# A hybrid encoder layer on one core: statistics and scaling of sv behind earlier tiles of u, and the multiplies by gffn behind later low parts

## The chip, the cores and the metric

The kernel runs on one core of a Trainium2 chip. A core has five engines with a queue each: TensorE (PE in the profile, its weight loads PEld), VectorE (DVE), ScalarE (ACT), GpSimd (POOL) and SyncE (SP), which here only issues DMAs. Each engine takes its instructions in the order of the program; an instruction that must wait for another engine holds all that stand behind it. The metric is the device time of one execution in microseconds (us), lower is better. All times before are of the kernel as it stands in the section after next.

## The reference, cut to what matters

One layer, 512 positions of width 1024, float32. The input projection yields eight pieces; the spatial gating unit (SGU) uses two of them, u and sv:

```
proj = h @ w_in
q, k, v, g, u, sv, a_ret, a_sgu = split(proj)

# SGU branch
u  = gelu(u)
sv = layernorm(gelu(sv), sgu_ln_g, sgu_ln_b)      # over the 1024 features of a position
mixed = einsum('gpq,bnqgc->bnpgc', w_spatial, sv by chunks of 128) + b_spatial
y_sgu = (u * mixed) @ w_sgu_o

merged = sigmoid(a_ret) * y_ret + sigmoid(a_sgu) * y_sgu
x  = x + rmsnorm(merged @ w_out) * g_post_mix
h2 = rmsnorm(x) * g_pre_ffn
f  = conv_gated_mlp(h2)                            # ends with (512 x 2816) @ w_down (2816 x 1024)
y  = x + rmsnorm(f) * g_post_ffn
```

The change touches two places: the layer norm of sv (its mean, variance and scaling, without the gain and bias, which are folded in later), and the multiply of f by g_post_ffn at the end.

## The kernel before, in words

**Products in split precision.** Every float32 operand of a product is split into a high part (a copy by ScalarE, rounded to TensorE's format, L97) and a low part (source minus high part, a subtraction by VectorE, L114). Each product is three matmuls: high by high, high by low, low by high. So each 512 KB block of weights costs a DMA, a split on ScalarE, a subtraction on VectorE, and then matmuls. Where a product is a 2 x 2 block product, the kernel uses a Strassen-like scheme with seven products of sums of blocks. The sums of weights (T1 to T4 at L196 to L202, and L217 to L222 for the last product) are VectorE's and in part POOL's.

**Buffers that pace the loads.** Weights are loaded into four buffers called raw (SyncE's queue), and their parts go into nine slots (names wh, wl, wf, sh, sl, dh, dl). A raw buffer is loaded anew when the last reader of the old content is done, a slot is written anew when TensorE has used it.

**The stage of u.** Four tiles of u are whole products (`f_block`, 24 matmuls of 128 x 512, j = 0 to 3 in the loop `for j in range(UW)`); four more come as two `Pair`s of seven-product form (matmuls of 128 x 256, L915). After a whole tile VectorE multiplies it by the row scale out of PSUM (L977) and ScalarE applies the gelu (L978). In a `Pair`, `part1` makes product 0, whose result ScalarE copies to c0; product 1, which VectorE adds to c0; S1 into a third bank; then S2 on top of bank 0 (so it must wait for the copy to c0), whose result ScalarE copies to c1. `part2` adds S3 on top of bank 0 (so it waits for the copy to c1) and copies again; `part3` ends the pair.

**sv.** The eight tiles svz[t, q] (t = 0 to 3 are the position chunks, q = 0, 1 the halves of the features) are ready before the stage of u. `sv_stats` takes their statistics (two BN_STATS and a BN_AGGR for each t, on VectorE), `sv_scale` turns mean and variance into a factor and a shift (one VectorE operation, then three POOL operations on 128 x 4), and `sv_norm(q)` applies them with one ScalarE operation for each t (L715, 128 x 512). sv is next read by `mix`, in the stage of the gates after u.

**Pass two of the last product.** The product by w_down runs in two passes of 512 output features, each over nine pairs of blocks (`products(m, j)`, j = 0 to 8; 42 matmuls each, L1351). Each j needs two units of weights: "q", three of four loaded blocks as they are (128 x 768), and "t", four sums of them (128 x 1024). In pass two, after j = 2 to 5, `first_share(t)` handles a chunk of pass one's result c: two squares with row sums on ScalarE, two multiplies by gffn (names zg<-c,gpf) and the sum of the row sums (q) on VectorE. zg is next read in `rows`, in the last 15 us.

**What sets the order.** The program is recorded in the order of the code, with `w_get` recording the loads, sums and splits of weights several units ahead of their use. A scheduler then orders each engine's queue. `tc.issue_after(i)` puts what is recorded under it behind instruction i on i's engine; it adds no wait between engines.

Of the kernel before, what the change touches and what calls it, by code (L numbers as in the profile page):

```python
# [18 lines left out]
NT = S // P  # L19
# [30 lines left out]
def tile_block(ctx: ExitStack, tc, xT, x, wall, par, cs, wsp, bsp, gpost, gffn, out):  # L50
    nc = tc.nc
# [10 lines left out]
    def blk(dt=F32, n="blk", shape=(P, S)):  # L62
        return sb.tile(list(shape), dt, tag="blk", bufs=NBLK, name=nm(n))
# [17 lines left out]
    def tmp(n="tmp", shape=(P, S)):  # L81
        return sb.tile(list(shape), F32, tag="tmp", bufs=6, name=nm(n))
# [13 lines left out]
    def copy(o, i):  # L96
        return nc.scalar.activation(out=o, in_=i, func=AF.Copy)  # L97

    def two(t):
        return t.rearrange("p (n c) -> p n c", n=2)  # L100
# [5 lines left out]
    def in_turn(o):  # L106
        return o.rearrange("p (c n) -> p n c", n=2)

    def as32(t):
        return t.bitcast(F32)  # L110

    def split(hi, lo, src):
        copy(hi, src)
        nc.vector.tensor_sub(lo, src, as32(hi))  # L114

# [4 lines left out]
    i = 0  # L122
    while i < NW:
        pair = [(f, i) for f in FORMS]
        if i == SV0:
# [3 lines left out]
            i = U0  # L129
# [6 lines left out]
        elif i == UP0 + 2 * COUPLES[0][0]:  # L136
# [3 lines left out]
            i = UP0 + 2 * COUPLES[-1][1] + 2  # L140
# [10 lines left out]
    v = nc.vector  # L151
# [11 lines left out]
    def w_block(i):  # L163
        raw = raw01[i] if i < 2 else raw_tile()
        resident = RES0 <= i < RES1
        if i > 1:
            nc.sync.dma_start(raw, wall[i])
        if resident:
            hi, lo = [], []
            for c in range(2):  # L170
                h_, l_ = blk(F32R, "wh"), blk(F32R, "wl")
                split(h_, l_, raw[:, c * S : (c + 1) * S])
                hi.append(h_)
                lo.append(l_)
        else:
            at = AT_192 if i >= DOWN0 else AT_64 if UP0 <= i < UP0 + EARLY else 0
            hi, lo = slot("wh", at), slot("wl", at)
            if i < 2:
                first_blocks(i, hi, lo, raw)
            else:  # L180
                with behind():
                    split(hi, lo, raw)
        return hi, lo

    def w_form(form, i):

        if form == "B11":
            a, b = raw_tile(), raw_tile()
            nc.sync.dma_start(a, wall[i])
            nc.sync.dma_start(b, wall[i + 1])  # L190
            w_raw["B11"], w_raw["B12"] = a[:, :S], a[:, S:]
            w_raw["B22"], w_raw["B21"] = b[:, :S], b[:, S:]
        elif form == "T1":
            t = raw_tile()
            w_raw["T1"], w_raw["T2"], w_raw["T3"], w_raw["T4"] = t[:, :S], t[:, S:], w_raw["B12"], t[:, S:]
            nc.vector.tensor_add(w_raw["T1"], w_raw["B11"], w_raw["B12"])  # L196
            nc.vector.tensor_add(w_raw["T3"], w_raw["B12"], w_raw["B22"])
            eng = nc.vector if i < GATE0 or i >= UP0 else nc.gpsimd
            eng.tensor_tensor(out=w_raw["T2"], in0=w_raw["T1"], in1=w_raw["B22"], op=ALU.add)
        elif form == "T4":  # L200
            eng = nc.vector if i < GATE0 or i >= UP0 else nc.gpsimd
            eng.tensor_tensor(out=w_raw["T4"], in0=w_raw["T2"], in1=w_raw["B21"], op=ALU.add)  # L202
        w = slot("wf", 0, 1088)
        lo, hi = w[:, AT_64 : AT_64 + S], w[:, S + AT_192 : 2 * S + AT_192]
        split(hi, lo, w_raw[form])
        return hi, lo
# [507 lines left out]
    def scaled_to(t, r, o):  # L714
        nc.scalar.activation(out=t, in_=t, func=AF.Identity, scale=r, bias=o)  # L715
# [77 lines left out]
    def sv_stats(ts):  # L793
        for t in ts:
            for nh in range(2):
                v.bn_stats(out=sst[:, t, nh, :], in_=svz[t, nh])
            v.bn_aggr(out=smv[:, t, :], in_=sst[:, t].rearrange("p a b -> p (a b)"))

    def sv_scale():
        v.tensor_scalar(out=sshift, in0=smv[:, :, 0], scalar1=-1.0, scalar2=None, op0=ALU.mult)  # L800
        rsqrt(srstd, smv[:, :, 1], 1.0, NT)
        shift(sshift, srstd)

    def sv_norm(q):
        for t in range(NT):
            scaled_to(svz[t, q], srstd[:, t : t + 1], sshift[:, t : t + 1])


# [78 lines left out]
    def f_block(ah, al, n, between=None):  # L887

        wh, wl = w_get()
        o = ps()  # L890
        for k in range(n):
            if between and k == n // 2:
                between()
            c = slice(k * P, (k + 1) * P)
            mm3(o, wh[:, c], wl[:, c], turns(ah[k]), turns(al[k]), k == 0, k == n - 1)
        return o
# [76 lines left out]
    for j in range(UW):  # L973
        with tc.issue_after(summed) if j == 0 else ExitStack():
            o = f_block(xh, xl, KD)
        u = U_HOMES.pop()()
        i = v.tensor_mul(two(u), in_turn(o), two(rbc)).ins  # L977
        g = nc.scalar.activation(out=u, in_=u, func=AF.Gelu_apprx_tanh).ins  # L978
        uT.append(u)
        with tc.issue_after(i):  # L980
            sv_stats(((0, 1), (2,), (3,), ())[j])
        if j == 2:
            sv_scale()
    with tc.issue_after(g):
        sv_norm(0)
    for j in range(UW // 2, KD // 2):
        p = Pair(AF.Gelu_apprx_tanh, lambda: U_HOMES.pop()(), None, rbc)
        p.part1()
        if late:
            late.part3()  # L990
        p.part2()
        late = p
        uT += p.t
        if j == UW // 2:
            with tc.issue_after(p.copied):
                sv_norm(1)
    yh, yl = [], []

    def mix(j):
# [310 lines left out]
    i = 0  # L1310
# [100 lines left out]
    gpf = []  # L1411
    qn = [small("q", 4, 4) for _ in range(NT)]
    zg = []

    def first_share(t):
        zg.append(blk(n="zg"))
        for i in range(2):
            src = c4[2 * (t // 2) + i][:, (t % 2) * 256 : (t % 2 + 1) * 256]
            j = tmp("junk")
            nc.scalar.activation(out=j[:, :256], in_=src, func=AF.Square, scale=D ** -0.5, accum_out=qn[t][:, 2 + i : 3 + i])  # L1420
            v.tensor_mul(zg[t][:, i * 256 : (i + 1) * 256], src, gpf[0][:, i * 256 : (i + 1) * 256])
        v.tensor_add(qn[t][:, 0:1], qn[t][:, 2:3], qn[t][:, 3:4])


# [88 lines left out]
    for j in range(DP):  # L1513
        products(m, j, steps if j == DP - 1 else {}, LOOK - (j == 0), freed[0] if j == 1 else None)
        if j == 0:
            gpf.extend((hi192("gpf", F32), lo64("gpf", F32)))
            for i in range(2):
                nc.gpsimd.dma_start(gpf[i], gffn[None, i * S : (i + 1) * S].to_broadcast([P, S]))
        if 1 < j < 2 + NT:
            first_share(j - 2)  # L1520
# [136 lines left out]
```

## Time and profile before

| what | value |
|---|---|
| three executions | 785.8, 786.5, 787.52 us (median 786.5) |
| the profiled execution | 787.56 us, of which the span of its instructions 785.8 us |
| granted TensorE clock, mean | 0.997 |
| TensorE matmuls, weight loads | 777.3 us (99% of the span), 720.5 us (92%) |
| VectorE, ScalarE, POOL | 626.2 us (80%), 467.2 us (59%), 104.4 us (13%) |
| the chain that ended last | 96% of it TensorE |
| the stage of u | about 199.7 to 237 us of the span |
| pass two of the last product | about 725 to 767 us of the span |

How to read it. The columns of a timeline are start, duration, engine, source line, operation, output<-input names, sizes and count, and in brackets the idle time of the engine just before and what ended it. In a list of groups the columns after the bar are total busy time, mean duration in ns, and total idle time before them. Matmuls are pipelined: the next one starts before the one before ends, so the time between two starts says more than a duration. In a table of windows each engine's busy time stands with its count of instructions, in the order TensorE, weight loads, VectorE, ScalarE, POOL, and behind them the granted clock, the DMA share and GB/s.

### The profile page before, as it was taken

The numbers are of one execution on the slowest core, as the hardware profiler recorded it, in microseconds if no ns is written. First come the engines' busy times: TensorE is split into PE (matmuls) and PEld (weight loads), VectorE is DVE, ScalarE is ACT, GpSimd is POOL, SyncE is SP. The second block draws the span as 40 slices with busy tenths as digits, with TensorE's granted clock in tenths as the row PEclk, the third lists the DMA queues.
The fourth block names the chain that finished last, engine by engine and source line by source line (L and its number), as shares of the span: only waits on it lengthen the run. The fifth ranks groups of instructions, "written<-read, shape, count | busy, mean of one in ns | idle before, by whom it ended". The sixth has DMA issues, their size and how long they took to land.

```text
span 785.8 us, 13253 instructions
## 1 busy us (share of the span) xinstructions
PE 777.3 (99%) x5067; PEld 720.5 (92%) x5067; DVE 626.2 (80%) x1067; ACT 467.2 (59%) x848; POOL 104.4 (13%) x132
## 2 busy tenths in 40 slices
PE   9999999999999999999999999999999999999996
PEld 8888998998899999999998898999999998999996
DVE  6467987788777877867765679989999889877887
ACT  6555558689375534444444776657777578744442
POOL 0040001130011111032210210001111012200001
PEclk9999999999999999999999999999999999999998
DMA  8782224463223333223349111435555365633244
GB/s 285 268 260 90 81 81 161 108 133 128 75 82 108 108 108 108 98 92 108 134 166 330 68 68 40 122 108 141 141 148 148 108 195 115 170 114 111 103 163 161
DMA packets 35888, 104.78 MB, mean 133 GB/s; under 512 B 4400, under 2 KB 6320, under 8 KB 35824
## 3 DMA queue, kind: packets, MB, share of 16 engines
q1 hardware_dynamic: 27936, 87.81, 32.6%
q0 software_dynamic: 7024, 14.95, 9.0%
q10 hardware_dynamic: 864, 1.18, 0.4%
q8 instruction: 39, 0.64, 0.3%
q14 instruction: 25, 0.20, 0.1%
HBM read 91.34 MB, written 4.19 MB: 122 GB/s over the span
## 4 chain that ended last, share of the span: by engine, by line
PE 96%; DVE 1%; ACT 1%; issue 1%; POOLq 0%; POOL 0%; DVEq 0%; ACTq 0%
PE ps L915 21%; PE ps L289 13%; PE ps L291 13%; PE ps L290 13%; PE ps L1351 10%; PE ps L744 5%; PE ps L623 4%; PE ps L625 4%; PE ps L624 4%; PE ps L1088 2%; PE ps L1086 2%; PE ps L1087 2%; PE ps L1367 2%; PE ps L1008 1%; PE ps L409 1%
## 5 line engine op out<-in xcount | busy, mean ns | idle before, releaser
L114 DVE TENSOR_TENSOR wl<-raw,wh 128x1024 fp32r<-128x1024 f32 (+1 forms) x88 | 100.6, 1152 | 55.6 <-issue 19.1
L97 ACT ACTIVATE wf<-raw 128x512 fp32r<-128x512 f32 x126 | 75.6, 623 | 85.8 <-PE ps L290 39.8
L97 ACT ACTIVATE wh<-raw 128x1024 fp32r<-128x1024 f32 (+2 forms) x92 | 89.2, 982 | 29.1 <-DMA raw<-wall 16.8
L915 PE MATMUL ps<-sh,wf 128*128 128x256 f32 x576 | 105.8, 276 | 0.5 <-ACT u L97 0.3
L114 DVE TENSOR_TENSOR wf<-raw,wf 128x512 fp32r<-128x512 f32 x126 | 92.3, 745 | 15.2 <-ACT wf L97 14.3
L915 PEld LDWEIGHTS ps<-sh,wf 128*128 128x128 f32 x576 | 91.8, 192 | 1.7 <-ACT u L97 1.1
L289 PE MATMUL ps<-h2h,wh 128*128 128x512 f32 (+1 forms) x256 | 90.6, 354 | 0.0
L290 PE MATMUL ps<-h2l,wh 128*128 128x512 f32 (+1 forms) x256 | 90.4, 353 | 0.0
L291 PE MATMUL ps<-h2h,wl 128*128 128x512 f32 (+1 forms) x256 | 90.4, 353 | 0.0
L915 PE MATMUL ps<-sl,wf 128*128 128x256 f32 x288 | 79.2, 275 | 0.0
L1351 PE MATMUL ps<-dl,fh 128*128 128x256 f32 x216 | 59.7, 276 | 0.3 <-DVE dl L114 0.3
L1351 PE MATMUL ps<-dh,fh 128*128 128x256 f32 x216 | 59.4, 275 | 0.0
L1351 PE MATMUL ps<-dh,fl 128*128 128x256 f32 x216 | 59.4, 275 | 0.0
L915 PEld LDWEIGHTS ps<-sl,wf 128*128 128x128 f32 x288 | 55.2, 192 | 0.4
L97 ACT ACTIVATE dh<-raw 128x768 fp32r<-128x768 f32 (+1 forms) x36 | 33.7, 951 | 35.7 <-DVE raw L222 21.8
L291 PEld LDWEIGHTS ps<-h2h,wl 128*128 128x128 f32 x256 | 48.6, 190 | 5.1
L289 PEld LDWEIGHTS ps<-h2h,wh 128*128 128x128 f32 x256 | 48.6, 190 | 4.5
L290 PEld LDWEIGHTS ps<-h2l,wh 128*128 128x128 f32 x256 | 48.6, 190 | 4.5
L625 PE MATMUL ps<-wh,xl 128*128 128x512 f32 x128 | 48.5, 379 | 0.0
L624 PE MATMUL ps<-wl,xh 128*128 128x512 f32 x128 | 48.5, 379 | 0.0
L623 PE MATMUL ps<-wh,xh 128*128 128x512 f32 x128 | 48.5, 380 | 0.0
L915 PE MATMUL ps<-xh,wf 128*128 128x256 f32 x240 | 44.0, 276 | 0.0
(343 smaller groups left out, 2187.3 us busy)
## 6 DMA issues: line engine op xcount, KB each, us to landing
raw<-wall SPq DMA_DIRECT2D x144, 512.0 KB, 3.6
x<-x SPq DMA_DIRECT2D x24, 256.0 KB, 5.6
fl<-gp POOLq DMA_DIRECT2D x12, 256.0 KB, 4.0
swap<-qkraw POOLq DMA_DIRECT2D x16, 128.0 KB, 4.3
x<-x POOLq DMA_DIRECT2D x8, 256.0 KB, 2.3
fl<-fs POOLq DMA_DIRECT2D x8, 256.0 KB, 3.3
xT<-xT SPq DMA_DIRECT2D x7, 256.0 KB, 5.3
xT<-xT POOLq DMA_DIRECT2D x4, 256.0 KB, 4.0
```

Source lines behind the costliest of these rows:

```text
L97: return nc.scalar.activation(out=o, in_=i, func=AF.Copy)
L114: nc.vector.tensor_sub(lo, src, as32(hi))
L289: nc.tensor.matmul(o, ah, bh, start=start, stop=False, skip_group_check=skip)
L290: nc.tensor.matmul(o, ah, bl, start=False, stop=False, skip_group_check=skip)
L291: nc.tensor.matmul(o, al, bh, start=False, stop=stop, skip_group_check=skip)
L623: nc.tensor.matmul(acc[t], xh[k][:, c], turns(wh[:, f]), start=k == 0, stop=False)
L624: nc.tensor.matmul(acc[t], xh[k][:, c], turns(wl[:, f]), start=False, stop=False)
L625: part_end[0] = nc.tensor.matmul(acc[t], xl[k][:, c], turns(wh[:, f]), start=False, stop=k == KD - 1)
L744: nc.tensor.matmul(bank[t], a_[:, c], turns(w_[:, f]), start=first and k == i == 0, stop=last and k == 3 and i == 2, skip_group_check=True,)
L915: self.last = nc.tensor.matmul(o, w_[:, c], a_, start=first and k == n == 0, stop=k == 3 and n == 2, skip_group_check=True,)
L1086: nc.tensor.matmul(o, ah, turns(bh), start=k == 0, stop=False)
L1351: nc.tensor.matmul(o, a_[:, c], turns(w_[:, f]), start=j == t == i == 0, stop=j == DP - 1 and i == 2 and n not in (M2, M3, M4), skip_group ...
```

## The change

The statistics of all four chunks are now taken behind the first two whole tiles of u instead of the first three, and factor and shift are made after the second. The scalings of half q = 0 are recorded behind the gelu of tile j = 2 (before: j = 3), two scalings of q = 1 behind the gelu of j = 3 and the other two behind the first copy to c1 (before: all four there). In pass two, each of the eight multiplies by gffn is recorded behind the low part that was recorded last, that is the low part of a unit of weights prepared ahead.

```diff
+    low = [None]
+
     def split(hi, lo, src):
         copy(hi, src)
-        nc.vector.tensor_sub(lo, src, as32(hi))
+        low[0] = nc.vector.tensor_sub(lo, src, as32(hi)).ins
...
-    def sv_norm(q):
-        for t in range(NT):
+    def sv_norm(q, ts=range(NT)):
+        for t in ts:
             scaled_to(svz[t, q], srstd[:, t : t + 1], sshift[:, t : t + 1])
...
         with tc.issue_after(i):
-            sv_stats(((0, 1), (2,), (3,), ())[j])
-        if j == 2:
+            sv_stats(((0, 1), (2, 3), (), ())[j])
+        if j == 1:
             sv_scale()
-    with tc.issue_after(g):
-        sv_norm(0)
+        if j > 1:
+            with tc.issue_after(g):
+                sv_norm(j - 2, range((NT, 2)[j - 2]))
...
             with tc.issue_after(p.copied):
-                sv_norm(1)
+                sv_norm(1, range(2, NT))
...
-            v.tensor_mul(zg[t][:, i * 256 : (i + 1) * 256], src, gpf[0][:, i * 256 : (i + 1) * 256])
+            with tc.issue_after(low[0]):
+                v.tensor_mul(zg[t][:, i * 256 : (i + 1) * 256], src, gpf[0][:, i * 256 : (i + 1) * 256])
```

The line numbers of the changed kernel are two to four higher. No instruction is added or removed. The queues of POOL and SyncE keep their order; those of ScalarE, VectorE and TensorE move at the places that follow. The numbers behind names tell tiles of one name apart, and may differ between the two kernels for the same tile.

First, ScalarE from the gelu of the third whole tile of u on. The row u<-ps is the copy to c0 of the first pair. Before:

```order
L978 ACTIVATE u_2324<-u_2324 128x512
L97 ACTIVATE wf_2342<-raw_2338 128x512
L97 ACTIVATE wf_2382<-raw_2339 128x512
L978 ACTIVATE u_2370<-u_2370 128x512
L715 ACTIVATE sv_1802<-sv_1802,sshift,srstd 128x512
L715 ACTIVATE sv_1803<-sv_1803,sshift,srstd 128x512
L715 ACTIVATE sv_2197<-sv_2197,sshift,srstd 128x512
L715 ACTIVATE sv_2199<-sv_2199,sshift,srstd 128x512
L97 ACTIVATE u_2377<-ps_2379 128x256
```

Now:

```order
L980 ACTIVATE u_2332<-u_2332 128x512
L717 ACTIVATE sv_1802<-sv_1802,sshift,srstd 128x512
L717 ACTIVATE sv_1803<-sv_1803,sshift,srstd 128x512
L717 ACTIVATE sv_2197<-sv_2197,sshift,srstd 128x512
L717 ACTIVATE sv_2199<-sv_2199,sshift,srstd 128x512
L97 ACTIVATE wf_2346<-raw_2342 128x512
L97 ACTIVATE wf_2384<-raw_2343 128x512
L980 ACTIVATE u_2374<-u_2374 128x512
L717 ACTIVATE sv_1978<-sv_1978,sshift,srstd 128x512
L717 ACTIVATE sv_1979<-sv_1979,sshift,srstd 128x512
L97 ACTIVATE u_2379<-ps_2381 128x256
```

The four scalings of q = 0 moved ahead of two splits and the last gelu; two scalings of q = 1, which stood after the copy to c1, now stand ahead of the copy to c0. Further on, the copy to c0 of the second pair moved ahead of one split. On TensorE three matmuls of the second pair, which stood between S1 and S2 of the first, now stand after S2, where four of the second pair follow.

Second, VectorE behind the product with the row scale of the second whole tile. Before:

```order
L114 TENSOR_TENSOR wf_2258<-raw_2251,wf_2258 128x512
L796 BN_STATS sst<-sv_2197 128x6
L796 BN_STATS sst<-sv_1912 128x6
L114 TENSOR_TENSOR wf_2292<-raw_2207,wf_2292 128x512
L797 BN_AGGR smv<-sst 128x2
L202 TENSOR_TENSOR raw_2251<-raw_2251,raw_2208 128x512
L977 TENSOR_TENSOR u_2324<-ps_2299,rbc_567 128x512
```

Now:

```order
L116 TENSOR_TENSOR wf_2258<-raw_2251,wf_2258 128x512
L798 BN_STATS sst<-sv_2197 128x6
L798 BN_STATS sst<-sv_1912 128x6
L798 BN_STATS sst<-sv_2199 128x6
L799 BN_AGGR smv<-sst 128x2
L798 BN_STATS sst<-sv_1913 128x6
L116 TENSOR_TENSOR wf_2300<-raw_2207,wf_2300 128x512
L799 BN_AGGR smv<-sst 128x2
L204 TENSOR_TENSOR raw_2251<-raw_2251,raw_2208 128x512
L802 TENSOR_SCALAR sshift<-smv 128x4
L979 TENSOR_TENSOR u_2332<-ps_2307,rbc_567 128x512
```

The last two statistics and the last aggregate came up from behind the third tile's product. The low part that reads raw_2207 stands behind them; it is that buffer's last reader, and SyncE's next load goes into it.

Third, VectorE in pass two, from the sums of one "t" unit (raw_8120) to the low part of the next (dl_8157). Before:

```order
L1421 TENSOR_TENSOR zg_8368<-c_7381,gpf_8116 128x256
L1421 TENSOR_TENSOR zg_8368<-c_7382,gpf_8116 128x256
L114 TENSOR_TENSOR dl_8125<-raw_8120,dh_8124 128x1024
L114 TENSOR_TENSOR dl_8131<-raw_8128,dh_8130 128x768
L217 TENSOR_TENSOR raw_8152<-raw_8128 128x512
L1422 TENSOR_TENSOR q_8047<-q_8047 128x1
L1421 TENSOR_TENSOR zg_8432<-c_7381,gpf_8116 128x256
L221 TENSOR_TENSOR raw_8152<-raw_8152,raw_8128 128x256
L1421 TENSOR_TENSOR zg_8432<-c_7382,gpf_8116 128x256
L222 TENSOR_TENSOR raw_8152<-raw_8152,raw_8128 128x256
L1422 TENSOR_TENSOR q_8048<-q_8048 128x1
L114 TENSOR_TENSOR dl_8157<-raw_8152,dh_8156 128x1024
```

Now:

```order
L1426 TENSOR_TENSOR q_8048<-q_8048 128x1
L224 TENSOR_TENSOR raw_8120<-raw_8120,raw_8082 128x256
L116 TENSOR_TENSOR dl_8125<-raw_8120,dh_8124 128x1024
L219 TENSOR_TENSOR raw_8152<-raw_8128 128x512
L116 TENSOR_TENSOR dl_8131<-raw_8128,dh_8130 128x768
L223 TENSOR_TENSOR raw_8152<-raw_8152,raw_8128 128x256
L224 TENSOR_TENSOR raw_8152<-raw_8152,raw_8128 128x256
L219 TENSOR_TENSOR raw_8208<-raw_8184 128x512
L116 TENSOR_TENSOR dl_8157<-raw_8152,dh_8156 128x1024
```

All eight multiplies left this stretch. They now stand two by two behind the low parts of the units after it, the first two behind the low part of the next "t" unit (dl_8213), the last two behind that of the last but one (dl_8405). The four row sums moved up ahead of the sums of raw_8120.

## The prediction

> **What bounds the kernel now.** I read the page first, then the two views of waits for TensorE (matmuls and weight loads apart), then the timelines of the two places that the change touches.
>
> ```profile
> PE 777.3 (99%) x5067; PEld 720.5 (92%) x5067; DVE 626.2 (80%) x1067; ACT 467.2 (59%) x848; POOL 104.4 (13%) x132
> ```
>
> TensorE sets the time: its matmuls fill 99% of the span. Only a place where TensorE stands still can give anything back, so I list those that belong to the change.
>
> ```profile
> PE ps L915 <- ACT u L97: 0.3, 1, 0.3
> PE ps L1351 <- DVE dl L114: 0.3, 1, 0.3
> ```
>
> ```profile
> PEld ps L915 <- ACT u L97: 1.1, 3, 0.5
> PEld ps L1351 <- DVE dl L114: 0.6, 2, 0.5
> ```
>
> The columns are total wait, times, longest. The matmul row shows 0.6 us, the weight loads 1.7 us for the same two causes: a copy of u by ScalarE, and a low part dl by VectorE. The truth is in the starts. TensorE's timeline in the stage of u:
>
> ```profile
> 224.71 0.28 PE L915 MATMUL ps<-xh,wf 128*128 128x256 f32 x1
> 225.31 0.38 PE L915 MATMUL ps<-sh,wf 128*128 128x256 f32 x1 [0.33 <-ACT u L97]
> 226.98 0.39 PE L915 MATMUL ps<-xh,wf 128*128 128x256 f32 x2
> 227.39 0.38 PE L915 MATMUL ps<-sh,wf 128*128 128x256 f32 x1
> 232.52 0.28 PE L915 MATMUL ps<-xl,wf 128*128 128x256 f32 x1
> 232.92 0.38 PE L915 MATMUL ps<-sh,wf 128*128 128x256 f32 x1
> ```
>
> Two in a row take 0.39 where one takes 0.28, so the step from one to the next is 0.11. A start that should come 0.11 after 224.71 comes 0.60 after it: 0.49 lost, and 0.10 more because the first matmul after a stop takes 0.38 instead of 0.28 (its weights were not loaded ahead). I call these stalls one to three: 0.59; 227.39 against 226.98 + 2 x 0.11, 0.19 + 0.10 = 0.29; 232.92 against 232.52 + 0.11, 0.29 + 0.10 = 0.39. Together 1.27 us.
>
> The second place, pass two of the last product:
>
> ```profile
> 740.95 0.28 PE L1351 MATMUL ps<-dh,fh 128*128 128x256 f32 x1
> 741.49 0.38 PE L1351 MATMUL ps<-dl,fh 128*128 128x256 f32 x1 [0.27 <-DVE dl L114]
> 746.29 0.38 PE L1351 MATMUL ps<-dl,fh 128*128 128x256 f32 x1
> 755.67 0.28 PE L1351 MATMUL ps<-dh,fh 128*128 128x256 f32 x1
> 755.93 0.38 PE L1351 MATMUL ps<-dl,fh 128*128 128x256 f32 x1
> ```
>
> By the same reckoning 0.43 + 0.10, then 0.10 alone, then 0.15 + 0.10: 0.88 us, always on the first matmul that reads a low part dl. So the whole stake is 1.27 + 0.88 = 2.15 us of 787.56, or 0.27%.
>
> The Trainium skill ("Perfetto Trace Analysis", section Identifying the Most-Contended Engine) says that matmul busy time misjudges TensorE because matmuls are pipelined, and that weight loads are the better measure. By the matmul row the stake would be 0.6 us, by the weight loads' 1.7; the starts side with the page.
>
> **Part one: statistics and scaling of sv.** ScalarE's timeline there:
>
> ```profile
> 216.38 0.61 ACT L978 ACTIVATE u<-u 128x512 f32<-128x512 f32 x1
> 220.50 1.15 ACT L97 ACTIVATE wf<-raw 128x512 fp32r<-128x512 f32 x2 [3.51 <-issue]
> 222.08 2.91 ACT L715 ACTIVATE sv<-sv,sshift,srstd 128x512 f32<-128x512 f32 x4
> 224.90 0.36 ACT L97 ACTIVATE u<-ps 128x256 f32<-128x256 f32 x1
> 226.96 0.38 ACT L97 ACTIVATE u<-ps 128x256 f32<-128x256 f32 x1
> 232.50 0.36 ACT L97 ACTIVATE u<-ps 128x256 f32<-128x256 f32 x1
> ```
>
> Four scalings of 2.91 us stand right ahead of the copy at 224.90, for which TensorE waits at 225.31 (stall one). Before 220.50 ScalarE sits idle for 3.51 us. The change puts the four into that hole. Whether they fit depends on the statistics:
>
> ```profile
> 211.51 1.28 DVE L796 BATCH_NORM_STATS2 sst<-sv 128x6 f32<-128x512 f32 x2
> 218.48 0.20 DVE L797 BATCH_NORM_AGGREGATE smv<-sst 128x2 f32<-128x12 f32 x1
> ```
>
> ```profile
> L114 DVE TENSOR_TENSOR wf<-raw,wf 128x512 fp32r<-128x512 f32 x126 | 92.3, 745 | 15.2 <-ACT wf L97 14.3
> ```
>
> ```profile
> 218.78 0.51 POOL L448 TENSOR_SCALAR rs<-smv 128x4 f32<-128x4 f32 x1 [42.93 <-DVE smv L797]
> 219.38 1.50 POOL L451 TENSOR_TENSOR srstd<-rs,nhalf 128x4 f32<-128x4 f32 x1
> 220.95 0.20 POOL L712 TENSOR_TENSOR sshift<-sshift,srstd 128x4 f32<-128x4 f32 x1
> ```
>
> From the last aggregate's start to the end of sshift is 221.15 - 218.48 = 2.67 us. Now four statistics run from 211.51 (2 x 1.28 = 2.56), with one aggregate (0.20) and one low part (0.75 in the mean of its group) before the last aggregate, which so starts at 215.0. Add 2.67: the scalings may start at 217.7, and the gelu of 216.38 is over by 217.0. They end at 217.7 + 2.9 = 220.6, just where the next splits begin (220.50). If they are late, the splits and the next gelu slip with them, and behind these two more scalings (half of 2.91, 1.46) and the copy: 222.08 + 1.46 + 0.36 = 223.9. TensorE now asks for the copy at 224.71 - 2 x 0.11 = 224.49, because the three matmuls that stood ahead of it in the old order come after it. So there is 0.6 us of cover behind the zero slack, and stall one goes: -0.59.
>
> The copy of stall two now waits for no scaling either before or after, and four matmuls stand between the product and the next use in both orders; the distance from copy (226.96) to matmul (227.39) is a latency. It stays: 0.00. Its bounds are 0.29 gone and 0.29 more.
>
> Stall three: the copy at 232.50 stands behind splits and the last scaling. It now moves ahead of one split. From a second copy at 226.96 - 0.92 (stall one's 0.59 and three matmuls' 0.33 no longer lie ahead of it) = 226.0, it has ahead of it two copies (0.74), two scalings (1.46), three splits (3 x 0.58): 230.0. TensorE asks 60 steps and one stall after 224.49: 224.49 + 60 x 0.11 + 0.29 = 231.4. Covered by 1.4 us: -0.39. Without that cover it keeps its 0.39.
>
> What is late next: on VectorE the low part that frees a raw buffer stands behind two more statistics. SyncE's queue waits for that buffer:
>
> ```profile
> 213.41 0.33 SPq L190 DMA_DIRECT2D raw<-wall  x1
> ```
>
> ```profile
> DMA to landing us min/median/max: 3.4/3.5/6.3
> ```
>
> ```profile
> 219.88 0.69 DVE L199 TENSOR_TENSOR raw<-raw,raw 128x512 f32<-128x512 f32 x1
> ```
>
> That load starts some 1.3 us later, at 214.7, and lands by the median at 218.2; of the two sums over it the second starts at 219.88, so the first is due near 219. At the maximum of 6.3 it would land at 221.0, some 1.6 us late for the following product with u, and the copy at 223.9 would become 225.5: stall one back as 225.5 - 224.5 = 1.0. I take the median: nothing else was issued near it.
>
> **Part two: the multiplies by gffn in pass two.** Busy time by window (its length, then TensorE, weight loads, VectorE, ScalarE, POOL), the group of multiplies, and the chain at the first stall:
>
> ```profile
> 725.00:739.10 14.10, 14.10 (x129) 14.10 (x128) 14.07 (x30) 5.55 (x17) 0.00 (x0) 1.00 0.22 76
> 739.10:748.50 9.40, 9.13 (x80) 8.90 (x80) 7.00 (x11) 3.59 (x4) 0.00 (x0) 1.00 0.32 112
> 748.50:757.80 9.30, 9.30 (x83) 9.13 (x82) 8.06 (x13) 5.51 (x6) 0.00 (x0) 1.00 0.36 118
> ```
>
> ```profile
> L1421 DVE TENSOR_TENSOR zg<-c,gpf 128x256 f32<-128x256 f32 x8 | 3.2, 421 | 0.0
> ```
>
> ```profile
> 738.61 0.42 DVE L222 TENSOR_TENSOR raw<-raw,raw 128x256 f32<-128x256 f32 x1
> 739.12 1.79 ACT L97 ACTIVATE dh<-raw 128x1024 fp32r<-128x1024 f32 x2 [3.70 <-PE ps L1351]
> 740.21 2.09 DVE L114 TENSOR_TENSOR dl<-raw,dh 128x1024 fp32r<-128x1024 f32 x2 [1.11 <-ACT dh L97]
> ```
>
> VectorE is full for 14 us (14.07 of 14.10), and all eight multiplies (3.2 us) lie in it, ahead of the last sum at 738.61. The sum ends at 739.03, the split starts at 739.12, so the wait charged to TensorE is really this sum's. Its low part starts at 740.21, takes some 1.2, and TensorE stops until 741.49. The change takes the eight out. What it exposes is one high part (half of 1.79, 0.9) for which VectorE will now wait, since it reaches that low part sooner. So the sum comes 3.2 - 0.9 = 2.3 us earlier by busy time; I count 1.4, since the multiplies' starts are only 0.34 apart (8 x 0.34 = 2.7) and the small row sums now wait for their squares. The need is 0.53: gone, with 0.9 to spare. The multiplies go, two at a time (0.84), behind later low parts, into stretches where VectorE idles 2.40 of 9.40 and 1.24 of 9.30. Each pair follows the low part that TensorE waited for (746.29, 755.93), so it can only delay the next one, 18 or 24 matmuls (2.0 or 2.6 us) later, and the lead won stays: -0.10 and -0.25. In all -0.88; the bounds are 0 and -0.88, plus 0.84 if one pair landed ahead of a tight low part.
>
> **Sum.** -0.59 - 0.39 - 0.88 = -1.86. Against the profiled execution, 787.56 (span 785.8 and 1.8 around it), 785.7. That execution is the slowest of the three; against their median of 786.5 it gives 784.6.
>
> **Rivals.** (a) Only pass two pays: ScalarE meets TensorE again in the stage of u, by a late load as above or a late start of the scalings. For it speaks the zero slack before 220.5; against it the 0.6 us behind. -0.88: 785.6. (b) Only recorded matmul idle comes back, 0.33 + 0.27 = 0.60: 785.9. For it speaks that the rest is inferred from starts; against it that steps of 0.11 hold everywhere else. (c) Slower: the three small POOL operations stand at the head of a chain that ScalarE's strict order now makes everything wait for. They move beside two-input sums of VectorE, and such company has been dear:
>
> ```profile
> 232.97 1.61 POOL L199 TENSOR_TENSOR raw<-raw,raw 128x512 f32<-128x512 f32 x1 [11.82 <-ACT u L97]
> 233.35 1.77 DVE L197 TENSOR_TENSOR raw<-raw,raw 128x512 f32<-128x512 f32 x1
> ```
>
> A sum that takes 0.69 alone (219.88 above) took 1.77 beside POOL's, 1.1 more. If each of the three were held so, the scalings would start 3.3 us late, at 221.0, and hold the splits, the gelu and the copy: 223.9 + 3.3 = 227.2 plus 0.4 to the matmul, 3.1 us after 224.5. With stalls two and three as before, the stage loses 2.6 more than before (3.1 + 0.1 for stall one, where it was 0.59); less 0.88, +1.7: 788.2. It decides from 0.6 us of lateness on. Against it: 219.88 lies inside POOL's 1.50 us and took its usual 0.69. The Trainium skill ("SBUF — State Buffer", section SBUF: two separate sides) says that VectorE operations with two SBUF inputs and GpSimd operations that read SBUF exclude each other for a whole instruction, by which (c) would happen at least in part; the row at 233.35 agrees, the one at 219.88 does not, for POOL operations of four elements.
>
> **How the numbers follow.** Forecast (784.6, its own range 784.2 to 785.2 by the bounds of stall two and of pass two) 0.66; (a) 0.20; (b) 0.07; (c) 0.07. The three runs lie 0.9 us to either side of their middle, so 0.2% (1.57 us, below which a measurement can't tell a change from none, under 784.93) cuts close to the forecast: some 0.8 of its chance and 0.15 of (a)'s fall below, 0.53 + 0.03 = 0.56 faster. Slower is (c), 0.07. The rest, 0.37, is within. The range takes the whole stake (786.5 - 2.15 = 784.35) less 0.75 for the runs, 783.6, to (a) and (b) plus 0.9, 786.6; it leaves out (c).
>
> **What would show it.** Right: scalings between 217 and 220.5 with the splits still at 220.5; no ScalarE wait on the weight loads of L917 but one; VectorE's last sum of that form near 737.6 and no wait on dl; the multiplies after 743. Wrong: scalings starting after 218.5, a raw load of the u stage landing after 220, or a new wait on dl after a pair of multiplies. Equal gaps in TensorE's starts with a time unchanged would say that the stalls were given back further on, where I see no wait now.

## The result and the profile after

| | before | after |
|---|---|---|
| median, 22 runs each | 786.36 us (785.44 to 787.81) | 785.19 us (784.34 to 785.97) |
| ratio, 95% interval | | 0.9984 [0.9978, 0.9990] |
| the profiled execution (span) | 787.56 us (785.8) | 785.08 us (783.3) |

The change saves 1.2 us (0.8 to 1.7 by the interval). The engines of the changed kernel, and the only weight load that still waits for a copy of u by ScalarE:

```profile
PE 775.6 (99%) x5067; PEld 720.3 (92%) x5067; DVE 626.5 (80%) x1067; ACT 467.8 (60%) x848; POOL 104.0 (13%) x132
```

```profile
PEld ps L917 <- ACT u L97: 0.2, 1, 0.2
```

Three such waits have become one. TensorE's timeline of the changed kernel shows which (lines have moved by two, L915 is L917):

```profile
225.53 0.28 PE L917 MATMUL ps<-xl,wf 128*128 128x256 f32 x1
225.64 0.39 PE L917 MATMUL ps<-xh,wf 128*128 128x256 f32 x2
226.06 0.38 PE L917 MATMUL ps<-sh,wf 128*128 128x256 f32 x1
```

226.06 comes 0.20 after its due time (225.64 + 2 x 0.11) and takes 0.10 more: stall two, 0.30 us. The other two are gone. What the stage gains can be read between the 1167th and the 1311th matmul, one ahead of the pairs and one behind the three stalls; first before, then after:

```profile
220.25 0.38 PE L291 MATMUL ps<-xh,wl 128*128 128x512 f32 x1
...
237.71 0.28 PE L915 MATMUL ps<-sh,wf 128*128 128x256 f32 x1
```

```profile
219.85 0.38 PE L293 MATMUL ps<-xh,wl 128*128 128x512 f32 x1
...
236.32 0.28 PE L917 MATMUL ps<-sh,wf 128*128 128x256 f32 x1
```

17.46 us became 16.47: 0.99 less. (In a second profile of the kernel before, the same stretch took 17.37, since its stall three was 0.29 and not 0.39; so the gain is 0.9 to 1.0.) The 0.40 by which the first row is earlier is no part of the gain: that matmul starts at 219.58 in the second profile of before, so its time differs by more than that between executions of one kernel. ScalarE in the stage of u (the last row is the copy of stall three), then the chain that lets its scalings start, on VectorE and POOL, all of the changed kernel:

```profile
216.60 2.92 ACT L717 ACTIVATE sv<-sv,sshift,srstd 128x512 f32<-128x512 f32 x4
220.05 1.15 ACT L97 ACTIVATE wf<-raw 128x512 fp32r<-128x512 f32 x2 [0.53 <-PE ps L292]
221.63 1.51 ACT L717 ACTIVATE sv<-sv,sshift,srstd 128x512 f32<-128x512 f32 x2
223.04 0.36 ACT L97 ACTIVATE u<-ps 128x256 f32<-128x256 f32 x1
...
229.37 0.36 ACT L97 ACTIVATE u<-ps 128x256 f32<-128x256 f32 x1
```

```profile
214.16 0.20 DVE L799 BATCH_NORM_AGGREGATE smv<-sst 128x2 f32<-128x12 f32 x1
214.27 0.64 DVE L204 TENSOR_TENSOR raw<-raw,raw 128x512 f32<-128x512 f32 x1
...
217.75 0.69 DVE L199 TENSOR_TENSOR raw<-raw,raw 128x512 f32<-128x512 f32 x1 [0.17 <-DMA raw<-wall]
```

```profile
214.46 0.51 POOL L450 TENSOR_SCALAR rs<-smv 128x4 f32<-128x4 f32 x1 [39.01 <-DVE smv L799]
215.05 1.04 POOL L453 TENSOR_TENSOR srstd<-rs,nhalf 128x4 f32<-128x4 f32 x1
216.17 0.27 POOL L714 TENSOR_TENSOR sshift<-sshift,srstd 128x4 f32<-128x4 f32 x1
```

The four scalings fill the hole from 216.60 to 219.52, and the splits behind them wait for TensorE, not for ScalarE. In pass two no weight load waits for a low part any more. The same three windows as in the prediction, VectorE around the old first stop, and TensorE at the matmul that stopped there:

```profile
725.00:739.10 14.10, 14.10 (x128) 14.10 (x128) 12.30 (x23) 7.35 (x19) 0.00 (x0) 1.00 0.30 109
739.10:748.50 9.40, 9.40 (x86) 9.40 (x86) 9.30 (x17) 3.60 (x4) 0.00 (x0) 1.00 0.31 120
748.50:757.80 9.30, 9.30 (x85) 9.30 (x85) 8.81 (x16) 4.74 (x6) 0.00 (x0) 1.00 0.40 132
```

```profile
736.17 0.42 DVE L224 TENSOR_TENSOR raw<-raw,raw 128x256 f32<-128x256 f32 x1
736.51 0.69 DVE L219 TENSOR_TENSOR raw<-raw 128x512 f32<-128x512 f32 x1
737.78 2.09 DVE L116 TENSOR_TENSOR dl<-raw,dh 128x1024 fp32r<-128x1024 f32 x2 [0.58 <-ACT dh L97]
...
743.25 0.75 DVE L1425 TENSOR_TENSOR zg<-c,gpf 128x256 f32<-128x256 f32 x2
```

```profile
739.38 0.28 PE L1354 MATMUL ps<-dh,fh 128*128 128x256 f32 x1
739.50 0.28 PE L1354 MATMUL ps<-dl,fh 128*128 128x256 f32 x1
```

The multiplies have left the first window (14.07 busy became 12.30) for the two behind it (7.00 became 9.30, 8.06 became 8.81). The first of the two low parts at 737.78 ends at 739.01, and the matmul that reads it starts on its beat at 739.50: half a microsecond to spare, where it was 0.38 late before (it ended at 741.44, and the matmul was due at 741.06).

### The profile page after: what moved, and what is told of

Read it like the earlier page. It is cut to its first block, busy times and chain, and to the rows that moved or that the text cites. A ratio compares the mean times of both kernels' runs of the same rounds, so it can differ in the third digit from the quotient of the medians.

```text
span 783.3 us, 13258 instructions
## 1 busy us (share of the span) xinstructions
PE 775.6 (99%) x5067; PEld 720.3 (92%) x5067; DVE 626.5 (80%) x1067; ACT 467.8 (60%) x848; POOL 104.0 (13%) x132
## 4 chain that ended last, share of the span: by engine, by line
PE 98%; DVE 1%; ACT 0%; POOLq 0%; issue 0%; POOL 0%; DVEq 0%
PE ps L917 22%; PE ps L291 13%; PE ps L293 13%; PE ps L292 13%; PE ps L1354 11%; PE ps L746 5%; PE ps L625 4%; PE ps L627 4%; PE ps L626 4%; PE ps L1089 2%; PE ps L1091 2%; PE ps L1090 2%; PE ps L1370 2%; PE ps L1011 1%; PE ps L411 1%; PE ps L393 0%
## 5 line engine op out<-in xcount | busy, mean ns | idle before, releaser
L917 PE MATMUL ps<-sh,wf 128*128 128x256 f32 x576 | 105.3, 275 | 0.0
L917 PEld LDWEIGHTS ps<-sh,wf 128*128 128x128 f32 x576 | 91.7, 192 | 0.8 <-ACT u L97 0.2
L917 PE MATMUL ps<-sl,wf 128*128 128x256 f32 x288 | 79.3, 275 | 0.0
L917 PEld LDWEIGHTS ps<-sl,wf 128*128 128x128 f32 x288 | 55.3, 192 | 0.4
L917 PE MATMUL ps<-xh,wf 128*128 128x256 f32 x240 | 43.8, 276 | 0.0
```

The source lines that it names most:

```text
L917: self.last = nc.tensor.matmul(o, w_[:, c], a_, start=first and k == n == 0, stop=k == 3 and n == 2, skip_group_check=True,)
```

## The experiments

Four sets, each beside runs of the kernel before on the same chip. All the times, in us; the difference is the ratio less one, times the median of before. The ratio is not the quotient of the two medians (part one alone has 786.38 to 786.37 and a ratio of 0.9997):

| kernel | median | before | ratio, interval | difference |
|---|---|---|---|---|
| part one alone | 786.38 | 786.37 | 0.9997 [0.9988, 1.0006] | -0.2 |
| part two alone | 786.15 | 786.37 | 0.9999 [0.9990, 1.0008] | -0.1 |
| before again | 786.61 | 786.37 | 1.0006 [0.9997, 1.0015] | +0.5 |
| the change again | 785.16 | 786.37 | 0.9987 [0.9978, 0.9996] | -1.0 |
| before, sums later | 786.67 | 786.66 | 0.9994 [0.9985, 1.0003] | -0.5 |
| part one, sums later | 786.02 | 786.66 | 0.9991 [0.9983, 1.0000] | -0.7 |
| the change, sums later | 785.35 | 786.66 | 0.9981 [0.9972, 0.9991] | -1.5 |
| part one alone, again | 785.86 | 786.66 | 0.9986 [0.9977, 0.9995] | -1.1 |
| before, low parts first | 786.27 | 786.65 | 0.9995 [0.9986, 1.0004] | -0.4 |
| part one, low parts first | 785.19 | 786.65 | 0.9981 [0.9972, 0.9990] | -1.5 |
| the change, low parts first | 785.34 | 786.65 | 0.9982 [0.9973, 0.9991] | -1.4 |
| part two alone, again | 786.05 | 786.45 | 0.9992 [0.9983, 1.0001] | -0.6 |

An interval is some 0.7 us to either side, so single differences under that tell little; the profiles have to carry the reading, and the repeats.

### Each part alone

Part one alone is the change without its last place, part two alone the change without its first:

```diff
-            with tc.issue_after(low[0]):
-                v.tensor_mul(zg[t][:, i * 256 : (i + 1) * 256], src, gpf[0][:, i * 256 : (i + 1) * 256])
+            v.tensor_mul(zg[t][:, i * 256 : (i + 1) * 256], src, gpf[0][:, i * 256 : (i + 1) * 256])
```

```diff
-            sv_stats(((0, 1), (2, 3), (), ())[j])
-        if j == 1:
+            sv_stats(((0, 1), (2,), (3,), ())[j])
+        if j == 2:
             sv_scale()
-        if j > 1:
-            with tc.issue_after(g):
-                sv_norm(j - 2, range((NT, 2)[j - 2]))
+    with tc.issue_after(g):
+        sv_norm(0)
...
-                sv_norm(1, range(2, NT))
+                sv_norm(1)
```

> Part one alone. My theory (the two parts are separate and each gives back its own stalls): in the stage of u only stall two is left, 0.29 us after the matmuls following the copy to c1, and all three stalls of pass two are still there (0.53, 0.10 and 0.25 us); time 0.98 us under the kernel before, ratio 0.9988. Rival 'one execution': the stalls of pass two were an accident of the execution that was profiled, so part one carries the whole measured gain of 1.2 us and pass two shows no stall here. Rival 'given back': the matmul starts of the u stage move up by 1 us, but the time is that of before, ratio 1.0000.

> Part two alone. My theory: the stage of u keeps its three stalls (0.59, 0.29, 0.39 us), pass two has none; time 0.88 us under the kernel before, ratio 0.9989. Rival 'one execution': pass two shows no stall here either, but the time is that of before, ratio 1.0000. Rival 'given back': no stall in pass two, time as before, with a new wait in the last 20 us.

> The kernel before, profiled once more. My theory: all six stalls appear again at the same matmuls and of the same size within 0.1 us (1.27 us in the stage of u, 0.88 us in pass two), since they come from the order of the queues; ratio 1.0000 within the interval. Rival 'one execution': the stalls of pass two, which depend on a sum that ended 0.09 us before the split it released, are absent or under half of 0.88 us.

> The changed kernel, profiled once more. My theory: stall two alone is left of the six (0.29 us), and the ratio is 0.9976 to 0.9984. Rival 'one execution': a stall of 0.2 us or more appears in one of the two places although it is not in the first profile.

In this set the two parts alone came out at before's time, both together at the change's. By the first theory they should have read 0.98 and 0.88 us less; both values lie just outside the intervals. (Later runs of the same two kernels gave -1.1 and -0.6, so by the times alone the parts may still add up: their means are -0.65 and -0.35 against the -1.0 to -1.2 of the change.) In the profile of part one alone the stage of u is as quick as in the changed kernel (stalls one and three gone), so the 1 us was won there. It is lost again at the end, in pass two, where TensorE now waits longer, most of it for low parts. The weight loads of part one alone, and TensorE's two largest stops there:

```profile
PEld ps L1352 <- DVE dl L114: 1.3, 4, 0.5
```

```profile
739.77 0.28 PE L1352 MATMUL ps<-dh,fh 128*128 128x256 f32 x1
740.39 0.38 PE L1352 MATMUL ps<-dl,fh 128*128 128x256 f32 x1 [0.34 <-DVE dl L114]
...
754.57 0.28 PE L1352 MATMUL ps<-dh,fh 128*128 128x256 f32 x1
754.93 0.38 PE L1352 MATMUL ps<-dl,fh 128*128 128x256 f32 x1
```

By starts 0.61 and 0.35; all its stops from 686 us on come to 1.9 (1.7 of it on matmuls that read a low part), against 0.88 in the first profile of before. The kernel before again has only 0.54 of them (0.25, 0.10 and 0.19 by starts; the expectations in the next section say 0.47), neither the same within 0.1 nor under half. The row of its weight loads shows one short wait:

```profile
PEld ps L1351 <- DVE dl L114: 0.2, 1, 0.2
```

So the size of this stop differs from execution to execution, and in this profile it is larger where TensorE arrives earlier. That suggests that something on VectorE's side keeps its own time. The changed kernel again has stall two and no stop on a low part, but it has a new one: 0.30 us at 727.50, where by the profile a weight load waits for VectorE's yy (L1391). The rival foresaw such a stop. Its ratio of 0.9987 is above the 0.9976 to 0.9984 that were expected, which its interval still holds.

### A load that VectorE waits for at 640 us

VectorE's first sum over the first load of the last product (L217) starts at 644.80 in the second profile of before and at 645.37 in part one alone, where TensorE is ahead; the load had been issued earlier (SyncE's rows), and took longer. First before again, then part one alone:

```profile
640.48 9.00 SPq L212 DMA_DIRECT2D raw<-wall  x2
644.80 0.68 DVE L217 TENSOR_TENSOR raw<-raw 128x512 f32<-128x512 f32 x1
```

```profile
639.52 10.53 SPq L212 DMA_DIRECT2D raw<-wall  x2
645.37 0.69 DVE L217 TENSOR_TENSOR raw<-raw 128x512 f32<-128x512 f32 x1 [1.44 <-DMA raw<-wall]
```

My first theory was that this wait is what takes the lead back. The edit moves the three sums of that load behind five small operations that are ready:

```diff
+    formed = [None]
...
-            nc.vector.tensor_tensor(
+            with tc.issue_after(formed[0]) if i == DOWN0 else ExitStack():
+                nc.vector.tensor_tensor(
...
-        v.tensor_add(a[:, T1], b[:, T0], s_[:, T1])
+        formed[0] = v.tensor_add(a[:, T1], b[:, T0], s_[:, T1]).ins
```

> The kernel before, with one move on VectorE: the three sums over the first load of the last product (a load of 512 KB issued at about 640 us) now stand behind the five small operations that stood between and behind them, all of which have their operands by then. In four of the six profiles so far VectorE idled 0.55 to 1.44 us ahead of the first of these sums, waiting for that load (0.83 in the profile of before), and in two it did not. Theory L (the load): the loss at this load is carried some 95 us through a VectorE that is nearly full, and comes out as TensorE's wait for low parts in pass two. Then VectorE idles under 0.2 us here, the stops of TensorE on low parts dl come to 0.5 us or less (they were 0.47 where the load was in time), and the median is 0.3 to 0.6 below before: 785.8 to 786.1. Theory V (VectorE's own work): the 14 full microseconds ahead of pass two alone make the stops. Then they stay between 0.47 and 0.9 us and the time is that of before within 0.2.

> Part one alone (the statistics and scalings of sv moved, pass two as before), with the same move of the three sums behind the small operations. Theory L: the 0.9 us by which part one lets TensorE run earlier were lost at the load, which does not come earlier with TensorE; with the wait gone they reach the end: stops on dl 0.5 us or less in sum, median 0.7 to 1.0 below the run of before with the sums moved, 784.9 to 785.4. Theory V: VectorE's work from 645 to 740 us does not shift with TensorE, so the lead is given back all the same: stops on dl of 1.3 us or more, median 786.2 to 786.5.

> The changed kernel with the same move of the three sums. Both theories: taking 3.2 us of multiplies out of VectorE's full stretch already covers up to 2.4 us of lateness, the changed kernel shows no stop on dl, so there is nothing left to win at the load: 785.0 to 785.3, within 0.2 of the changed kernel. A gain of more than 0.4 us would say that the load costs by a way that neither theory has.

> Part one alone once more, word for word the kernel of the first run of it, for the spread of its profile. Theory L: the stops on dl in pass two are about 0.5 us plus what VectorE idled ahead of the first sum (1.44 us in the first profile of it, with 1.9 us of stops), whatever that idle is this time; median 786.2 to 786.5. Theory N (part one's gain is real and the first look an accident): stops on dl of 0.5 us or less, median 785.4 to 785.8.

The wait went, but the theory fell. Before with the sums later has no stop on a low part, as the theory asked, yet its median of 786.67 is that of before; in its profile stall three was 0.83 us instead of 0.39, which takes back half a microsecond. Part one with the sums later still has a stop on a low part (0.72 us by starts, with what follows it), and its median of 786.02 is above the 784.9 to 785.4 that the theory asked for. It is below the 786.2 to 786.5 of theory V as well. Its weight loads:

```profile
PEld ps L1355 <- DVE dl L114: 0.5, 1, 0.5
```

Part one alone again gave 785.86, between what the two theories said of it, with 1.2 us of stops on low parts and near them. That size fits theory L (0.5 and the 0.60 us that VectorE idled at the load this time), the median does not. The changed kernel with the sums later came out at 785.35, as both theories had it. This wait is at most a share.

### A ring of loads from 697 to 720 us

The waits of VectorE between 690 and 722 us, in the first profile of before:

```profile
DVE raw L217 <- DMA raw<-wall: 9.2, 5, 2.4
```

VectorE stands still five times there, 9.2 us in all, while TensorE works on. In the order of VectorE's queue one sees why (part one alone):

```profile
699.45 1.22 DVE L114 TENSOR_TENSOR wl<-raw,wh 128x1024 fp32r<-128x1024 f32 x1
703.03 0.69 DVE L217 TENSOR_TENSOR raw<-raw 128x512 f32<-128x512 f32 x1 [2.36 <-DMA raw<-wall]
703.64 0.95 DVE L114 TENSOR_TENSOR dl<-raw,dh 128x768 fp32r<-128x768 f32 x1
704.51 0.42 DVE L221 TENSOR_TENSOR raw<-raw,raw 128x256 f32<-128x256 f32 x1
704.96 0.42 DVE L222 TENSOR_TENSOR raw<-raw,raw 128x256 f32<-128x256 f32 x1
...
708.08 0.69 DVE L217 TENSOR_TENSOR raw<-raw 128x512 f32<-128x512 f32 x1 [1.56 <-DMA raw<-wall]
```

The low part at 703.64 is the last reader of its raw buffer, and the load that refills this buffer, for which the next of these sums waits, goes out only when it is done: it ends at 704.59, SyncE issues the load at 704.62, the load lands at 707.99, and the sum starts at 708.08. Its copy was made long before, by ScalarE:

```profile
696.80 0.85 ACT L97 ACTIVATE dh<-raw 128x768 fp32r<-128x768 f32 x1 [0.18 <-DMA raw<-wall]
```

So it could have run in the 2.36 us of waiting. Instead it stands behind the sum that waits, and the next load is late too: VectorE waits for a load, and the load for VectorE. TensorE is not in this ring, so a lead of TensorE should not make it run earlier. (At the 4000th matmul TensorE is 0.96 us earlier in part one alone than in before again, 645.35 against 646.31; the last sum ahead of the stop ends no earlier, at 737.92 against 737.77.) The edit puts such low parts ahead of the sums of four units; `split` now returns its subtraction:

```diff
+    low_q = []
+
     def w_down(form, i):
...
-            nc.vector.tensor_tensor(
+            with tc.issue_after(low_q[-2]) if i - DOWN0 in (7, 10, 11, 12) else ExitStack():
+                nc.vector.tensor_tensor(
...
-        split(hi, lo, raw)
+        ins = split(hi, lo, raw)
+        if form == "q":
+            low_q.append(ins)
```

> The kernel before with one change of order on VectorE between 697 and 720 us. There, in every profile so far, VectorE stands five times for 1.4 to 2.5 us ahead of the first sum over a load, while the low part that frees the buffer of the load after next stands behind that sum, its copy long done. The low parts now stand ahead of those sums. Theory R (a ring of loads): four buffers, VectorE waits for a load, and the load after that waits for VectorE; this ring sets its own pace, does not start earlier when TensorE does, and hands its lateness to pass two. With the ring opened the five waits shrink from some 9 us in sum to under 5, the stops of TensorE on low parts go (0.5 to 0.9 us in the profiles of before; 0.1 or less here), and the time falls by the mean of these stops: 0.4 to 0.9 below before, 785.6 to 786.2. Theory V (VectorE's own 14 full microseconds from 725 on): the waits may shrink, but the stops stay at 0.4 us or more and the time within 0.2 of before.

> Part one alone with the low parts ahead of the sums as well. Theory R: the 0.9 to 1.0 us that part one saves in the stage of u now reach the end, since the ring no longer takes them back: no stops on low parts, and 0.8 to 1.0 below the kernel before with the low parts first; 784.7 to 785.4. Theory V: stops on low parts of 0.7 us or more as in all three profiles with part one alone (0.7, 1.2 and 1.9), and 785.9 to 786.4.

> The changed kernel with the low parts ahead of the sums. Theory R: part two had already made room for the ring's lateness (no stops on low parts in three of three profiles of it but 0.3 us of one), so the ring is worth nothing more here: 784.9 to 785.3, within 0.2 of the changed kernel, and within 0.3 of part one alone with the low parts first. Theory V says the same of this kernel. If it is over 0.4 faster than the changed kernel, the ring costs by a way that was not seen.

> Part two alone once more, word for word the kernel of the first run of it (786.15 against 786.37, ratio 0.9999), to halve the doubt on its size. By the forecast's term, 0.88 from the one profile of before, it would read 785.7 to 785.9 against 786.6. By theory R, with the stops on low parts of the kernel before at 0 to 0.9 us, mean 0.45 over three profiles (one of them with three sums moved at the load of 640 us): 786.0 to 786.4, no stops on low parts, and stalls one to three of the stage of u as before.

VectorE in part one with the low parts first, its waits between 690 and 722 us and its timeline:

```profile
DVE raw L220 <- DMA raw<-wall: 3.1, 3, 1.5
DVE dl L114 <- PE ps L1357: 2.1, 3, 1.1
DVE dl L114 <- PE ps L1373: 1.4, 1, 1.4
```

```profile
700.09 1.22 DVE L114 TENSOR_TENSOR wl<-raw,wh 128x1024 fp32r<-128x1024 f32 x1
701.22 0.95 DVE L114 TENSOR_TENSOR dl<-raw,dh 128x768 fp32r<-128x768 f32 x1
703.62 0.69 DVE L220 TENSOR_TENSOR raw<-raw 128x512 f32<-128x512 f32 x1 [1.45 <-DMA raw<-wall]
...
706.55 0.69 DVE L220 TENSOR_TENSOR raw<-raw 128x512 f32<-128x512 f32 x1 [0.19 <-DMA raw<-wall]
...
710.31 1.23 DVE L114 TENSOR_TENSOR dl<-raw,dh 128x1024 fp32r<-128x1024 f32 x1 [1.40 <-PE ps L1373]
```

The low part runs before the sum, the next load is in time (issued at 702.20, landed at 706.46, a wait of 0.19), and from 710 on VectorE waits for TensorE: the ring is open and TensorE leads again. In the profiles of all three kernels with this edit no weight load waits for a low part, though in two of them the eight multiplies stand where they stood before. Part one then gains 785.19 - 786.27 = -1.08 us over before with the edit, about as much as it wins in the stage of u, and its median equals that of the whole change (785.19). The two ratios lie 1.1 us apart, each with some 0.7 us to either side, so this gain is only just clear, and it can't be told by times from the -0.2 to -1.1 of part one with the ring closed. Before with the edit came out at 786.27, a little above the 785.6 to 786.2 of theory R and not clear of no change. On top of the change the edit brings nothing (785.34 against 785.16 to 785.35), since there the multiplies had already made room. Had VectorE's own 14 full microseconds ahead of that sum been the limit, as the rival theory had it, part one would have stayed at 785.9 or more. The windows say the same: in the 14.00 us ahead of that sum VectorE is busy for 13.75 (before) and 13.79 (part one) with the ring open and no stop, 13.96 in both with it closed.

One number compares all profiles: by how much the low part of the first stop (739.50 in the changed kernel) was ready ahead of the time its matmul was due, 0.11 us after the matmul before it. A stop shows only what is below zero.

| kernel (each profile) | ahead of need, us |
|---|---|
| before; again; sums later | -0.38; -0.10; +0.57 |
| part one; again; sums later | -0.46; -0.45; -0.45 |
| part two; again | +1.06; +0.93 |
| the change; again; sums later | +0.48; +0.49; +1.42 |
| low parts first: before; part one; the change | +1.06; +1.06; +2.27 |

With part one alone the margin is negative in every profile. Moving the multiplies brings it from -0.45 to +0.48, opening the ring instead brings it to +1.06, both together to +2.27. Part two alone, in both its profiles, has the three stalls of the stage of u and no stop on a low part. It came out at 786.05 the second time, inside theory R's 786.0 to 786.4 and above the 785.7 to 785.9 of the forecast's term. No kernel was found that is faster than the changed one.

## Why the prediction was right, and what in it was not

- **Stalls one and three: right, in size too.** -0.59 - 0.39 = -0.98 was forecast, 0.99 measured between the two fixed matmuls. Stall two stayed, as said (0.29 forecast, 0.30 measured). The copies ended where the forecast had them: 223.40 (223.9 forecast) and, for stall three, 229.73 (230.0).
- **The start of the scalings: earlier than forecast** (216.60, not 217.7). This execution was 0.40 ahead by then, and from the first statistic to the last aggregate it took 3.05 us (211.11 to 214.16), where I had added up whole durations, 3.51; VectorE's starts are closer together than that, the low part for one took 0.60 and not the mean of 0.75. So the last aggregate came at 214.16 and not at 215.0. POOL's power of 128x4 took 1.04 us where it had taken 1.50. The slack ahead of the splits was not zero but 0.53 us.
- **The late raw load: right.** Its first reader started at 217.75 (218.2 forecast). The reader was not due near 219, as I had it: it stood ready and waited 0.17 us for the load, which cost TensorE nothing.
- **Pass two: the mechanism right, the size not.** The last sum ended at 736.59 and the multiplies began at 743.25, in the idle stretches; no stop on a low part is left. That is 2.4 us earlier than in the first profile of before, but executions of before differ (737.77 in the second). Against part one alone (737.92), which differs from the changed kernel by the multiplies only, it is 1.3 us earlier; 1.4 was forecast. The margin of 0.9 us is what part two alone has (1.06 and 0.93); in the changed kernel half of it is left, since part one lets TensorE come earlier there. But "In all -0.88" came from one execution: two other profiles with pass two in the old order have 0.54 (before again) and none (before with the sums later), a mean of 0.47 over the three. Part two alone gave -0.1 and -0.6 by its two ratios. With 0.47 for 0.88 the forecast's sum is -1.45, inside the measured -0.8 to -1.7.
- **The sum as a sum: not quite.** I added the two parts as if each had its own end. In the three profiles with part one and pass two in the old order (the third with the sums later), TensorE's stops at the end come to 1.9, 1.2 and 0.7 us, mean 1.3, against 0.47 without part one: 0.8 of the 1 us is given back there, by three profiles each. What I had called a sign against the forecast, stalls "given back further on, where I see no wait now", is what part one does alone. By the times the two runs of it (-0.2 and -1.1) are too far apart to show this; the profiles show it, and the 1.08 us that part one gains with the ring open agree with it.
- **Rivals.** (a) fell: the stage of u pays in full. (b) fell: stall one returned 0.59, not the 0.33 recorded. (c) fell: the three POOL operations took 0.51, 1.04 and 0.27, no more than before in sum, and VectorE's two-input sum beside them (214.27) took 0.64. The Trainium skill ("SBUF — State Buffer", section SBUF: two separate sides) has VectorE operations with two SBUF inputs and GpSimd operations that read SBUF exclude each other, so that one of them waits. In these rows VectorE did not wait, but POOL did, which agrees with the page for one of the two sides. The first operation took 0.51 us beside a two-input sum, in both orders, where 0.20 is enough with none beside it (116.19 in the profile of before); it ended at 214.97, just behind the sum (214.91). The power took 1.50 where such a sum (219.27 to 219.96) covered its start, 1.95 beside a longer one (172.63, the subtraction of 128x1024 that ends at 173.68), and 1.04 in the new order. The distances between POOL's starts say the same (0.59 against 0.29 for the first operation, 1.57 against 1.12 for the power). So what (c) feared exists, but its size was wrong: in the new order one of the three operations was held, by 0.3 us and not 1.1, and it had been held before too. What the prediction set against it, the 0.69 of the row at 219.88, tells of VectorE alone. No run was made to test this.
- **The base.** The profiled execution of before was 1.2 us above its kernel's median of 22 runs (787.56 against 786.36). Setting the sum against the median was right; taking the stops of that execution as typical was not.
- **The numbers.** The measured -1.2 us is two thirds of the -1.86 forecast, and the term of pass two is where most of the rest lies. The bounds of stall two (0.29 to either side) and of pass two (0 to 0.88) give 784.3 to 785.8 around 784.6, not the 784.2 to 785.2 that I wrote. And I gave 0.56 to a median below 784.93; it is 785.19.

## What to carry to other kernels

Price a small stop from several profiles of the same kernel, since one execution can overstate what can be won (0.88, 0.54 and 0 us here). Read not only the stop but the margin: how far ahead of its reader an operand is ready. When the bounding engine gains a lead, look downstream for a ring that does not contain it (buffer, load, another engine): there the lead can be handed back, unless that ring is opened or given slack. A ready instruction that frees a load's buffer belongs ahead of one that waits for a load.

## What was not expected of the hardware

- The same 512 KB load, issued at about 640 us, took 5.85 us to its first reader in one execution (639.52 to 645.37) and 4.32 at most in another (640.48 to 644.80).
- The same POOL power of 128x4 took 1.50 us in all six profiles with the statistics in the old order and 1.04 in all eight with the new one: it goes with the order, not with the execution.
- A stop of TensorE near 506 us, ahead of another pair, is as large as the whole gain in some executions and absent in others, of the same program. Part one alone again has it; the first run of that kernel has no such row:

```profile
PEld ps L915 <- ACT c L97: 1.1, 1, 1.1
```

Its cause was not tried.
